# A hybrid decoder block on one core: the order of the projection blocks and the spread of the time-mixing steps

## The chip, the core and the metric

The kernel runs on one core of a Trainium2 chip. The metric is the device time of one execution in microseconds (us). Engines are TensorE (PE, with its weight loads as PEld), VectorE (DVE), ScalarE (ACT), GpSimd (POOL) and SyncE (SP), whose queue issues most DMAs. The granted clock of TensorE is given as a share of full speed.

## What is computed

A decoder block for a sequence of 2048 positions and a width of 1024, in float32. One projection feeds two groups of heads: eight heads of RWKV-7 time mixing (a recurrence over time with a 64 x 64 state per head) and four heads of differential attention. Their outputs are concatenated and projected, and a gated MLP with a causal convolution follows.

```python
# D_MODEL 1024, SEQ 2048, 8 time-mixing heads of 64, 4 attention heads of 2 x 64, D_FF 2816, CONV_WIDTH 3
def rwkv7_mix(p, mu, ...):
    ...
    xs = p + (token_shift(p) - p) * mu
    r, k, v, w_lo, a_lo, g_lo = jnp.split(xs, cuts, axis=-1)
    decay = jnp.exp(-DECAY_SCALE * jax.nn.sigmoid(w_decay0 + jnp.tanh(w_lo) @ w_decay_up))
    a = jax.nn.sigmoid(w_iclr0 + a_lo @ w_iclr_up)
    g = jax.nn.sigmoid(g_lo) @ w_gate_up
    ...
    def step(state, inp):
        r_t, w_t, k_t, v_t, kk_t, a_t = inp
        sa = jnp.einsum('bhvk,bhk->bhv', state, -kk_t)
        state = (state * w_t[:, :, None, :]
                 + sa[..., None] * (kk_t * a_t)[:, :, None, :]
                 + v_t[..., None] * k_t[:, :, None, :])
        return state, jnp.einsum('bhvk,bhk->bhv', state, r_t)
    ...
    return y * g

def diff_attention(q, k, v, lam, slopes):
    ...
        s = jnp.einsum('bhcqd,bhckd->bhcqk', qblk.astype(jnp.float32), kh) * scale
        s = s - slopes[None, :, None, None, None] * dist
        s = jnp.where(dist >= 0, s, NEG_INF)
        pr = jax.nn.softmax(s, axis=-1)
        attn = pr[:, :, 0] - lam * pr[:, :, 1]
        return jnp.einsum('bhqk,bhkv->bhqv', attn, vh)
    ...

def reference(x, ...):
    ...
        xn = rms_norm(h, ln_attn_pre[l])
        proj = xn @ w_in[l]
        y_rwkv = rwkv7_mix(proj[..., :RWKV_COLS], ...)
        dq, dk, dv = jnp.split(proj[..., RWKV_COLS:], 3, axis=-1)
        ...
        o = diff_attention(dq, dk, dv, lam, slopes)
        o = rms_norm(o, diff_subln[l], eps=SUBLN_EPS) * (1.0 - lam_init)
        mix = jnp.concatenate([y_rwkv, o.reshape(B, S, DIFF_DIM)], axis=-1).astype(h.dtype)
        h = h + rms_norm(mix @ w_out[l], ln_attn_post[l])
        hn = rms_norm(h, ln_ffn_pre[l])
        u = causal_dwconv(hn @ w_up[l], conv_w[l], conv_b[l])
        gate, val = jnp.split(u, 2, axis=-1)
        f = (jax.nn.gelu(gate, approximate=True) * val) @ w_down[l]
        h = h + rms_norm(f, ln_ffn_post[l])
    return h
```

## The kernel before

**Products.** A float32 product is made of three matmuls with operands split into a high and a low part (L99, L100, L101; the weights are split in L92 and L93).

**Projections** (class Proj). The columns of w_in are taken in 26 blocks of 128: blocks 0 to 13 (NRW = 14) are time mixing's, blocks 14 to 25 (NDF = 12) attention's, three for each head. The sequence is taken in two halves of 1024 rows, since only one half of the normalized and transposed x (tiles xh and xl) is held at a time. `start` normalizes and transposes half 0 and runs blocks 0 and 1 as a pair; `prepare` normalizes one tile of half 1 and stores it to DRAM (xn); `second` loads these eight tiles, transposes and splits them (L84) into the same buffers. A block's results go to DRAM: rw for time mixing (with the token shift), qq, kk and vT for attention.

**Time mixing** (class Rwkv) works on 16 groups of 128 positions, in steps that a generator hands out, one per turn; there are TURNS = 132. A group g has `prepare` (4 turns: operands from rw, then the matrices M), `invert` (1: a chain of 62 dependent VectorE operations on tile X, L530 and L532, then DMAs through the DRAM tile xdr to M, bdx and x1t), `join` (1: matmuls into xp) and `scan` (2: matmuls rp, sp, yp and up, two chunks in a row, each on the state that the one before left). The steps of `post(g-1)` (gate, normalization, output) are run inside scan(g). After nine first turns the plan is, for each g: join(g), scan(g), prepare(g+2), invert(g+1). `need` is the highest group that the next step wants, so that it is not run before that group's half has been projected.

**Attention** (class Attn) runs 64 units, four heads of 16 query blocks of 128. `scores` of unit i are followed by `output` of unit i - LAG (LAG = 2). VectorE evicts the scores (E, L794), ACT takes the exponential, TensorE transposes E (tp, L827), ACT copies the result (at, L829) and TensorE multiplies by V (op, L833); POOL ends a unit (on, L840). PSUM holds four banks in one set (tag MM) and two sets of two (RA, RC). Time mixing uses the sets of two; units below ALONE = 40 take everything from the set of four, later units use RA for transposes and RC for outputs.

**The order before.** Half 0: blocks 0 to 13, then 14 to 25 with `prepare` of half 1 in the first eight of them; `second`; half 1: blocks 0 to 25. Through the attention blocks of half 0 and the time-mixing blocks of half 1 the generator gives 1.5 turns for each block (PER), from then on 3.5 (PER2), 81 in all when the projections end. The other 51 turns are spread evenly over the first SPREAD = 44 attention units. When the last turn is done the weights of the output projection are loaded and split (tiles wor, woh, wol) and the convolution's tables cvA and cvB are made.

The program is built with `schedule_with_timeline_sim=True`: a scheduler moves instructions within each engine's order, so the order of the code is a wish and not the final order. Each engine then runs its own rows in order.

Of the kernel before, what the change touches and what calls it, by code (L numbers as in the profile page):

```python
# [8 lines left out]
F32 = mybir.dt.float32  # L9
# [8 lines left out]
P = 128  # L18
D = 1024
S = 2048  # L20
KB = D // P
HALF = 1024
GRP = 512
NRW = 14
NDF = 12
# [100 lines left out]
class Proj:  # L126


    def __init__(self, tc, nc, cx, I, pool):
        self.tc, self.nc, self.cx, self.I, self.pool = tc, nc, cx, I, pool  # L130
        ps = cx.ps
        self.rk = ["k_k", "k_a", "ln_x_w", "ln_x_b"]
        self.gain = None
        self.carry = pool.tile([P, NRW], F32, name="carry", bufs=1)
        nc.vector.memset(self.carry, 0.0)
        self.w_in = I["w_in"][0].rearrange("(kb p) c -> p kb c", p=P)
        self.half = 0

    def tables(self):
        nc, cx, I = self.nc, self.cx, self.I  # L140
# [7 lines left out]

    def begin(self, half):
        self.half = half  # L150
        self.xh, self.xl = alloc_xhl(self.pool, f"x{half}")

    def load(self, t, first=None):

        nc, pool = self.nc, self.pool
        if first:
            xt = self.norm(t, first, 8)
        else:
            xt = pool.tile([P, D], F32, name=f"xn{t}", tag="xt", bufs=2)
            nc.sync.dma_start(xt, self.cx.xn[t])  # L160
        transpose_split(nc, self.cx, self.cx.ps, xt, self.xh, self.xl, t, *(RA if first else MM))

    def second(self):
        self.begin(1)
        for t in range(HALF // P):
            self.load(t)

# [8 lines left out]

    def prepare(self, t):

        xt = self.norm(HALF // P + t, self.pool, 2)
        self.nc.sync.dma_start(self.cx.xn[t], xt)  # L180

    def weights(self, cb):
# [893 lines left out]


TURNS = 2 * 4 + 1 + NGRP * 3 + (NGRP - 2) * 4 + NGRP - 1 + 4
PER, PER2, SPREAD = 1.5, 3.5, 44


def block_kernel(tc, I, out):
    nc = tc.nc
    cx = Ctx()
    with ExitStack() as st:
# [6 lines left out]
        cx.kk = dt("kk", [NH, 2, 130, S])  # L1092
        cx.vT = dt("vT", [NH, P, S])
        cx.mix = [dt(f"mix{g}", [8, P, GRP]) for g in range(S // GRP)]
        cx.xn = [dt(f"xn{t}", [P, D]) for t in range(HALF // P)]
        cx.h = dt("hres", [S, D])
        cx.hn = dt("hnorm", [HALF, D])
        setup_consts(tc, nc, cx)
# [3 lines left out]
        with pool("pj", "left") as pp:  # L1102
            pj = Proj(tc, nc, cx, I, pp)
            with pool("x0", "right") as xp:
                pj.start(xp)
            attn_consts(tc, nc, cx, I)
            cx.const = right.enter_context(pool("const2", "right"))
            rwkv_consts(tc, nc, cx, I)
            rw = Rwkv(tc, nc, cx, right.enter_context(pool("rk", "right")), cx.ps)
            steps = rw.steps()  # L1110
            need = next(steps)
            turns = 0
            for cb in range(2, NRW):
                pj.block(cb)
            block = lambda cb: lambda: pj.block(cb)
            work = [block(cb) for cb in range(NRW, NRW + NDF - 2)]
            for t in range(HALF // P):
                f = work[t]
                work[t] = lambda f=f, t=t: (f(), pj.prepare(t))
            work += [lambda: pj.pair(NRW + NDF - 2, NRW + NDF - 1), lambda: pj.second()]  # L1120
            work += [lambda: pj.pair(0, 1), lambda: None] + [block(cb) for cb in range(2, NRW + NDF)]
            due = NDF + NRW
            for i, f in enumerate(work):
                upto = PER * (i + 1) if i < due else PER * due + PER2 * (i + 1 - due)
                while turns < upto and (need < HALF // RG or i >= due):
                    need = next(steps)
                    turns += 1
                f()
# [39 lines left out]
```

## Time and profile before

| what | value |
|---|---|
| median of 3 runs | 3182.57 us (3182.32 to 3184.49) |
| profiled execution | 3163.65 us |
| its span | 3161.9 us |
| TensorE busy | 3027.9 us, 96% of the span |
| VectorE busy | 1912.3 us, 60% |
| ScalarE busy | 1168.6 us, 37% |
| last projection matmul | 828.18 us |
| last time-mixing matmul | 1348.16 us |
| last attention unit ends | 1498.95 us |

The program has four stretches: projections up to 828 us, with time mixing between their matmuls from about 190 us on; attention with the rest of time mixing up to 1349; attention alone up to 1499.6; then the output projection and the MLP. A share of busy time is an average over these, so each is read by itself below. In the timeline a row gives the start, the duration, the engine, the line, the operation, the tile written and the tiles read; a wait before it stands in brackets with what ended it.

### The profile page before, as it was taken

To read this page: it belongs to the slowest core of one execution; us is meant where nothing else is said; L and a number is where in the kernel's file an instruction comes from. 1 tells how busy PE (TensorE), PEld (TensorE's weight loads), DVE (VectorE), ACT (ScalarE), POOL (GpSimd) and SP (SyncE) were. 2 spreads that over 40 slices of the span, in tenths; PEclk is the share of its full clock that TensorE was granted. 3 is DMA by queue.
4 is the path that set the end of the run, shared out by engine and by line. 5 is a ranking of instruction groups with operands and counts; after the bars stand their busy time and mean duration, and the time that the engine had idled before them with its cause. 6 is when DMAs were issued, how large, how long until landed. Compare 5 with 4: busy or idle time off the path is not lost.

```text
span 3161.9 us, 46143 instructions
## 1 busy us (share of the span) xinstructions
PE 3027.9 (96%) x17347; PEld 2489.9 (79%) x17347; DVE 1912.3 (60%) x4898; ACT 1168.6 (37%) x2332; POOL 328.2 (10%) x441
## 2 busy tenths in 40 slices
PE   7999999999988898889999999999999999999998
PEld 6887778787767777778888888888887888888886
DVE  5246655566588787777555455555557465555556
ACT  4233323333365655577333222222224322222223
POOL 3000000010232323232000000000000000000002
PEclk9999999999899998989999999999999999999999
DMA  5346523345623525152444111111114211111112
GB/s 156 97 147 182 164 89 104 95 112 135 140 65 74 101 64 97 43 140 60 146 160 153 47 54 51 50 47 41 57 51 162 78 47 40 55 53 47 47 34 87
DMA packets 362208, 282.41 MB, mean 89 GB/s; under 512 B 96847, under 2 KB 308402, under 8 KB 361986
## 3 DMA queue, kind: packets, MB, share of 16 engines
q1 hardware_dynamic: 334898, 247.12, 26.6%
q0 software_dynamic: 24784, 28.16, 5.0%
q10 hardware_dynamic: 2304, 4.20, 0.4%
q8 instruction: 137, 2.24, 0.3%
q14 instruction: 85, 0.70, 0.1%
HBM read 204.72 MB, written 73.88 MB: 88 GB/s over the span
## 4 chain that ended last, share of the span: by engine, by line
PE 78%; DVE 6%; DMA 3%; ACT 1%; issue 1%; SPq 1%; POOL 0%; DVEq 0%; ACTq 0%; POOLq 0%
PE fp L99 10%; PE fp L101 10%; PE fp L100 10%; PE dn L100 5%; PE dn L99 5%; PE dn L101 5%; PE pp L100 4%; PE pp L99 4%; PE pp L101 4%; PE op L833 3%; PE po L99 2%; PE po L101 2%; PE po L100 2%; PE sp L789 1%; PE sp L790 1%
## 5 line engine op out<-in xcount | busy, mean ns | idle before, releaser
L1015 DVE TENSOR_TENSOR acc<-dn,acc 128x512 f32<-128x512 f32 x320 | 211.5, 687 | 224.4 <-PE dn L101 222.1
L99 PE MATMUL fp<-f1h,uh 128*128 128x512 f32 x704 | 275.4, 391 | 5.0 <-DVE fcarry L980 5.0
L101 PE MATMUL fp<-f1h,ul 128*128 128x512 f32 x704 | 275.3, 391 | 0.0
L100 PE MATMUL fp<-f1l,uh 128*128 128x512 f32 x704 | 275.3, 391 | 0.0
L100 PE MATMUL dn<-dl,gh 128*128 128x512 f32 x704 | 275.2, 391 | 0.0
L99 PE MATMUL dn<-dh,gh 128*128 128x512 f32 x704 | 272.4, 391 | 1.9 <-DVE acc L1015 1.9
L99 PE MATMUL fp<-f0h,uh 128*128 128x512 f32 x704 | 274.2, 389 | 0.0
L101 PE MATMUL fp<-f0h,ul 128*128 128x512 f32 x704 | 274.1, 389 | 0.0
L100 PE MATMUL fp<-f0l,uh 128*128 128x512 f32 x704 | 274.0, 389 | 0.0
L101 PE MATMUL dn<-dh,gl 128*128 128x512 f32 x704 | 264.0, 391 | 0.0
L93 DVE TENSOR_TENSOR ul<-ur,uh 128x1024 fp32r<-128x1024 f32 x88 | 107.7, 1225 | 188.1 <-ACT uh L92 188.1
L794 DVE TENSOR_SCALAR_CACHE_REDUCE E<-sp 128x512 f32<-128x512 f32 (+3 forms) x320 | 187.4, 605 | 41.7 <-PE sp L792 23.9
L976 DVE SCALAR_TENSOR_TENSOR u<-fp,cvA,u 128x511 f32<-128x511 f32 x176 | 131.3, 746 | 119.8 <-ACT u L974 119.8
L833 PE MATMUL op<-V,at 128*128 128x128 f32 x1088 | 161.5, 294 | 29.2 <-ACT at L829 28.4
L92 ACT CAST dh<-dr 128x1024 fp32r<-128x1024 f32 x44 | 44.4, 1047 | 386.8 <-PE dn L101 383.9
L833 PEld LDWEIGHTS op<-V,at 128*128 128x128 f32 x1088 | 143.6, 202 | 42.6 <-ACT at L829 35.9
L100 PE MATMUL pp<-x1l,wh 128*128 128x512 f32 x416 | 168.7, 406 | 0.0
L99 PE MATMUL pp<-x1h,wh 128*128 128x512 f32 x416 | 168.3, 405 | 0.0
L99 PE MATMUL pp<-x0h,wh 128*128 128x512 f32 x416 | 167.9, 404 | 0.1
L803 ACT ACTIVATE E<-E,asc 128x1024 f32<-128x1024 f32 (+7 forms) x160 | 153.6, 963 | 37.1 <-DVE asc L799 36.6
L100 PE MATMUL pp<-x0l,wh 128*128 128x512 f32 x416 | 167.3, 402 | 0.0
L101 PE MATMUL pp<-x0h,wl 128*128 128x512 f32 x416 | 167.0, 402 | 0.0
(303 smaller groups left out, 6697.5 us busy)
## 6 DMA issues: line engine op xcount, KB each, us to landing
ur<-in_w_up SPq DMA_DIRECT2D x88, 512.0 KB, 3.8
wr<-in_w_in SPq DMA_DIRECT2D x52, 512.0 KB, 4.3
dr<-in_w_down SPq DMA_DIRECT2D x44, 512.0 KB, 3.4
rw<-e SPq DMA_DIRECT2D x56, 256.0 KB, 3.9
x<-in_x SPq DMA_DIRECT2D x16, 512.0 KB, 6.1
qq<-e SPq DMA_DIRECT2D x64, 128.0 KB, 2.3
kk<-e SPq DMA_DIRECT2D x64, 128.0 KB, 2.4
ab<-adr SPq DMA_DIRECT2D x64, 128.0 KB, 2.7
```

The source lines that it names most:

```text
L92: nc.scalar.copy(wh, wr)
L93: nc.vector.tensor_tensor(wl, wr, wh.bitcast(F32), op=ALU.subtract)
L99: nc.tensor.matmul(out, lh(kb), rh(kb), start=(kb == 0), stop=False)
L100: nc.tensor.matmul(out, lh(kb), rl(kb), start=False, stop=False)
L101: nc.tensor.matmul(out, ll(kb), rh(kb), start=False, stop=(kb == n - 1))
L789: nc.tensor.matmul(sp[:, 0:n], qa[:, c, qs], ka[:, c, 0:n], start=True, stop=False)
L790: nc.tensor.matmul(sp[:, 0:n], qx[0:66, c, qs], kb[0:66, c, 0:n], start=False, stop=not last)
L794: nc.vector.tensor_scalar(e[ch * GRP // EW][:, eo:eo + n], sp[:, 0:n], -1.0, None, op0=ALU.mult, op1=ALU.min, accum_out=mx[:, ch:ch + 1])
L803: nc.scalar.activation(e[i][:, 0:n], e[i][:, 0:n], AF.Exp, bias=nm, scale=-1.0, accum_out=z)
L833: nc.tensor.matmul(op, at[:, q, :], v[:, q, :], start=(kb == 0), stop=(kb == qb))
L976: stt(u[:, 1:GRP], pp[:, 0:GRP - 1], w1(b), u[:, 1:GRP], op0=ALU.mult, op1=ALU.add)
L1015: nc.vector.tensor_tensor(acc[:, t, ds_], po, acc[:, t, ds_], op=ALU.add)
```

## The change

Half 0 runs only its 14 time-mixing blocks first (with `prepare` of half 1 in eight of them); then `turn(1)` loads half 1, which runs its 14 time-mixing blocks and its 12 attention blocks; then `turn(0)` loads half 0 a second time, and its 12 attention blocks end the projections. For that `start` also stores the eight tiles of half 0 to xn, which now has 16 tiles. `uses` only numbers names. Turns are given out from the first block of half 1 on: 57 (FIRST) up to the end of its time-mixing blocks, 126 (DONE) at the end of all blocks; the last six go to the first six attention units (SPREAD).

```diff
--- before.py
+++ after.py
@@ -134,7 +134,7 @@
         self.carry = pool.tile([P, NRW], F32, name="carry", bufs=1)
         nc.vector.memset(self.carry, 0.0)
         self.w_in = I["w_in"][0].rearrange("(kb p) c -> p kb c", p=P)
-        self.half = 0
+        self.half = self.uses = 0
 
     def tables(self):
         nc, cx, I = self.nc, self.cx, self.I
@@ -148,6 +148,7 @@
 
     def begin(self, half):
         self.half = half
+        self.uses += 1
         self.xh, self.xl = alloc_xhl(self.pool, f"x{half}")
 
     def load(self, t, first=None):
@@ -155,13 +156,16 @@
         nc, pool = self.nc, self.pool
         if first:
             xt = self.norm(t, first, 8)
+            nc.sync.dma_start(self.cx.xn[t], xt)
         else:
-            xt = pool.tile([P, D], F32, name=f"xn{t}", tag="xt", bufs=2)
-            nc.sync.dma_start(xt, self.cx.xn[t])
+            n = self.half * (HALF // P) + t
+            xt = pool.tile([P, D], F32, name=f"xn{self.uses}_{n}", tag="xt", bufs=2)
+            nc.sync.dma_start(xt, self.cx.xn[n])
         transpose_split(nc, self.cx, self.cx.ps, xt, self.xh, self.xl, t, *(RA if first else MM))
 
-    def second(self):
-        self.begin(1)
+    def turn(self, half):
+
+        self.begin(half)
         for t in range(HALF // P):
             self.load(t)
 
@@ -176,7 +180,8 @@
 
     def prepare(self, t):
 
-        xt = self.norm(HALF // P + t, self.pool, 2)
+        t += HALF // P
+        xt = self.norm(t, self.pool, 2)
         self.nc.sync.dma_start(self.cx.xn[t], xt)
 
     def weights(self, cb):
@@ -1076,7 +1081,7 @@
 
 
 TURNS = 2 * 4 + 1 + NGRP * 3 + (NGRP - 2) * 4 + NGRP - 1 + 4
-PER, PER2, SPREAD = 1.5, 3.5, 44
+FIRST, DONE, SPREAD = 57, 126, 6
 
 
 def block_kernel(tc, I, out):
@@ -1092,7 +1097,7 @@
         cx.kk = dt("kk", [NH, 2, 130, S])
         cx.vT = dt("vT", [NH, P, S])
         cx.mix = [dt(f"mix{g}", [8, P, GRP]) for g in range(S // GRP)]
-        cx.xn = [dt(f"xn{t}", [P, D]) for t in range(HALF // P)]
+        cx.xn = [dt(f"xn{t}", [P, D]) for t in range(S // P)]
         cx.h = dt("hres", [S, D])
         cx.hn = dt("hnorm", [HALF, D])
         setup_consts(tc, nc, cx)
@@ -1110,18 +1115,24 @@
             steps = rw.steps()
             need = next(steps)
             turns = 0
-            for cb in range(2, NRW):
+            for cb in range(2, NRW - 2):
                 pj.block(cb)
+                if cb - 2 < HALF // P:
+                    pj.prepare(cb - 2)
+            pj.pair(NRW - 2, NRW - 1)
+            pj.turn(1)
             block = lambda cb: lambda: pj.block(cb)
-            work = [block(cb) for cb in range(NRW, NRW + NDF - 2)]
-            for t in range(HALF // P):
-                f = work[t]
-                work[t] = lambda f=f, t=t: (f(), pj.prepare(t))
-            work += [lambda: pj.pair(NRW + NDF - 2, NRW + NDF - 1), lambda: pj.second()]
-            work += [lambda: pj.pair(0, 1), lambda: None] + [block(cb) for cb in range(2, NRW + NDF)]
-            due = NDF + NRW
+            pair = lambda cb: [lambda: pj.pair(cb, cb + 1), lambda: None]
+            last = NRW + NDF - 2
+            work = pair(0) + [block(cb) for cb in range(2, NRW)]
+            due = len(work)
+            work += [block(cb) for cb in range(NRW, last)] + pair(last)
+            work += [lambda: (pj.turn(0), pj.pair(NRW, NRW + 1)), lambda: None]
+            work += [block(cb) for cb in range(NRW + 2, NRW + NDF)]
             for i, f in enumerate(work):
-                upto = PER * (i + 1) if i < due else PER * due + PER2 * (i + 1 - due)
+                upto = FIRST * min(i + 1, due) / due
+                if i >= due:
+                    upto += (DONE - FIRST) * (i + 1 - due) / (len(work) - due)
                 while turns < upto and (need < HALF // RG or i >= due):
                     need = next(steps)
                     turns += 1
```

From L200 on, lines of the changed kernel stand five below those of before (L607 is L612, L560 is L565, L789 is L794). In the rows that follow, pp is a projection block, up, rp, sp_N, yp with one number belong to the scan of that group, gp, mp and vs to post, n and bo to prepare, xp to join; sp_ABC of a score row is made of head and query block and chunk, as tp and op of transposes and outputs.

TensorE at the end of projections, before: behind the last rows of block 25 of half 1 stand the last products of scan 7 (up_7) and the join of group 8.

```order
L99 MATMUL pp_25_1_8169<-x1h_3129,wh_25_8137 128x512
L100 MATMUL pp_25_1_8169<-x1l_3131,wh_25_8137 128x512
L101 MATMUL pp_25_1_8169<-x1h_3129,wl_25_8138 128x512
L607 MATMUL up_7_7266<-sav_6345,bkt_6355 64x64 x8
L644 MATMUL gp_7287<-sg_5630,gup 128x128 x4
L366 MATMUL n_9_7322<-rT_556,sel 128x128 x4
L560 MATMUL xp_7597<-ident,x1t_7595 128x32 x4
L590 MATMUL rp_8_7688<-state_588,AR_6769 64x64 x8
L565 MATMUL xp_7597<-x_8_7598,bda 128x32 x4
```

TensorE at the same place after: the block is that of half 0 (x0h), and behind it stand up_10 and the join of group 11.

```order
L99 MATMUL pp_25_1_10541<-x0h_8054,wh_25_10509 128x512
L100 MATMUL pp_25_1_10541<-x0l_8056,wh_25_10509 128x512
L101 MATMUL pp_25_1_10541<-x0h_8054,wl_25_10510 128x512
L468 MATMUL bo_8013<-t_b_8010,ones_551 128x512
L612 MATMUL up_10_7908<-sav_6925,bkt_6935 64x64 x8
L649 MATMUL gp_7929<-sg_6138,gup 128x128 x4
L371 MATMUL n_12_7964<-rT_572,sel 128x128 x4
L565 MATMUL xp_8453<-ident,x1t_8451 128x32 x4
L595 MATMUL rp_11_8472<-state_604,AR_7349 64x64 x8
L570 MATMUL xp_8453<-x_11_8454,bda 128x32 x4
```

Three more groups stand ahead of this point than before, five are still to come (11 to 15).

TensorE some 130 rows later, after: the last scores of unit 6 (sp_611), then the join of group 12 and its scan.

```order
L794 MATMUL sp_611_11045<-ka_10878,qa_11021 128x384
L795 MATMUL sp_611_11045<-kb_10879,qb_11022 128x384
L797 LDWEIGHTS identb
L797 MATMUL sp_611_11045<-caus,identb 128x128
L565 MATMUL xp_8981<-ident,x1t_8979 128x32
L595 MATMUL rp_12_9072<-state_604,AR_7949 64x64 x8
L565 MATMUL xp_8981<-ident,x1t_8979 128x32 x3
L570 MATMUL xp_8981<-x_12_8982,bda 128x32 x4
L573 MATMUL xp_8981<-bdx,x_12_8988 32x128 x4
L600 MATMUL sp_12_9082<-kv_8352,M_8016 64x64 x8
L632 MATMUL mp_9093<-ybv_7351,ones_551 128x512
L609 MATMUL yp_12_9098<-AR_7949,state_604 64x64 x8
```

From here on no row of attention stands on TensorE for 108 rows, up to this place (gp and vs are the last rows of post 15, tp_50 and op_5 belong to unit 5, sp_700 to unit 7):

```order
L639 MATMUL vs_10846<-onesmc,t_a_10808 128x2 x4
L649 MATMUL gp_10982<-sg_9808,gup 128x128 x4
L366 MATMUL vs_10846<-ident,rs_ln_10851 8x128
L371 MATMUL vs_10846<-rT_573,sel 128x128 x4
L48 MATMUL cvA_ps<-ident,cvA_st 128x128
L48 MATMUL cvB_ps<-ident,cvB_st 128x128
L832 MATMUL tp_50_11118<-ident,E_500_10952 128x128 x4
L838 MATMUL op_5_11117<-V_10578,at_50_11123 128x128 x4
L832 MATMUL tp_51_11129<-ident,E_500_10952 128x128 x2
L794 MATMUL sp_700_11146<-ka_10573,qa_11021 128x512
```

Before, the last row of post 15 stood among the outputs of units 43 and 44 (head 2, query blocks 11 and 12):

```order
L827 MATMUL tp_111_13989<-ident,E_1100_13748 128x128 x4
L644 MATMUL gp_13909<-sg_12318,gup 128x128 x4
L827 MATMUL tp_112_14000<-ident,E_1101_13749 128x128 x4
L827 MATMUL tp_120_14073<-ident,E_1200_13856 128x128 x4
L833 MATMUL op_11_13977<-V_12417,at_110_13983 128x128 x4
L833 MATMUL op_11_13977<-V_12842,at_111_13994 128x128 x4
```

The time-mixing rows of groups 12 to 15 have moved out from between the attention units to a place of their own ahead of unit 7.

VectorE in that place, after: in the chain of group 13 (X, xtmp) stands the addition kv_12, which reads rp_12, the first product of scan 12.

```order
L535 TENSOR_TENSOR xtmp_9503<-X_8783,ab_8778 128x66
L537 TENSOR_TENSOR X_8783<-X_8783,xtmp_9503 128x3x22
L535 TENSOR_TENSOR xtmp_9503<-X_8783,ab_8778 128x63
L597 TENSOR_TENSOR kv_8352<-rp_12_9072,kv_8352 128x256
L537 TENSOR_TENSOR X_8783<-X_8783,xtmp_9503 128x3x21
L535 TENSOR_TENSOR xtmp_9503<-X_8783,ab_8778 128x60
```

Forty rows of the chain stand behind this addition.

Behind the last time-mixing row the eight splits of the output weights (wol) stand on VectorE ahead of the first eviction of unit 7 there; before, five of them stood ahead of the evictions of unit 45 and three among these.

TensorE in `turn(0)`, after (xt are the transposes of x; vt and bt belong to prepare 8):

```order
L84 MATMUL xt_0_8075<-ident,xn_1_8073 128x128 x3
L84 MATMUL xt_1_8082<-ident,xn_1_8073 128x128 x4
L570 MATMUL xp_5921<-x_7_5922,bda 128x32 x4
L497 MATMUL vt_5798<-ident,vv_5614 128x128 x4
L506 MATMUL bt_8_5808<-ident,BK_5622 128x128 x4
L84 MATMUL xt_0_8091<-ident,xn_2_8089 128x128 x4
L84 MATMUL xt_1_8098<-ident,xn_2_8089 128x128 x4
```

As in `second` before, time-mixing rows stand between the transposes; in `turn(1)` there are none, since no turn has been given out by then.

## Rows read from the trace of the kernel before

**Rows 1.** Windows: busy us (x instructions) of PE, PEld, DVE, ACT, POOL; PEclk, DMA, GB/s.

```profile
600.00:828.40 228.40, 228.40 (x1818) 183.43 (x1816) 142.73 (x418) 80.23 (x168) 22.69 (x21) 1.00 0.46 115
828.40:913.00 84.60, 72.04 (x586) 59.77 (x586) 59.74 (x205) 39.67 (x106) 33.24 (x45) 0.78 0.58 119
828.40:1349.00 520.60, 456.04 (x4026) 382.41 (x4026) 400.88 (x1477) 296.92 (x753) 152.66 (x202) 0.90 0.40 82
1366.00:1386.00 20.00, 18.76 (x51) 13.24 (x52) 19.16 (x53) 12.13 (x19) 1.50 (x2) 0.50 0.24 76
1413.00:1499.60 86.60, 81.37 (x592) 71.91 (x590) 69.17 (x253) 68.73 (x173) 27.71 (x43) 1.00 0.22 63
```

**Rows 2.** Windows, projection matmuls alone (tile pp): PE busy (count), clock, DMA share, GB/s.

```profile
600.00:828.40 228.40, 154.34 (x606) 1.00 0.46 115
```

**Rows 3.** PE timeline, end of projections: start, us, engine, line, operation, tiles, count.

```profile
827.02 0.39 PE L99 MATMUL pp<-x1h,wh 128*128 128x512 f32 x1
...
828.18 0.40 PE L101 MATMUL pp<-x1h,wl 128*128 128x512 f32 x1
```

**Rows 4.** PE timeline, last block of half 0, `second`, first matmul of half 1.

```profile
372.76 0.39 PE L101 MATMUL pp<-x0h,wl 128*128 128x512 f32 x1
...
380.69 1.94 PE L84 MATMUL xt<-ident,xn 128*128 128x128 f32 x8 [1.88 <-DMA xn<-xn]
...
397.49 1.09 PE L84 MATMUL xt<-ident,xn 128*128 128x128 f32 x8 [1.46 <-DMA xn<-xn]
...
398.34 0.48 PE L99 MATMUL pp<-x1h,wh 128*128 128x512 f32 x1
```

**Rows 5.** DVE timeline, first and last operation of two inverse chains.

```profile
788.84 0.19 DVE L530 TENSOR_TENSOR xtmp<-X,ab 128x31 f32<-128x31 f32 x1 [2.68 <-DMA ab<-adr]
...
809.49 0.18 DVE L532 TENSOR_TENSOR X<-X,xtmp 128x8 f32<-128x8 f32 x1
...
863.52 0.18 DVE L530 TENSOR_TENSOR xtmp<-X,ab 128x31 f32<-128x31 f32 x1
...
913.05 0.18 DVE L532 TENSOR_TENSOR X<-X,xtmp 128x8 f32<-128x8 f32 x1
```

**Rows 6.** SP and PE timelines: load of x1t behind an inverse, join of its group.

```profile
924.51 0.43 SPq L547 DMA_DIRECT2D x1t<-xdr  x1
...
926.82 0.24 PE L560 MATMUL xp<-ident,x1t 32*128 32x32 f32 x1
```

**Rows 7.** PE timeline, first rp and last up of two scans.

```profile
831.17 0.68 PE L590 MATMUL rp<-state,AR 64*64 64x64 f32 x16
...
868.95 0.69 PE L607 MATMUL up<-sav,bkt 128*64 128x64 f32 x16
...
1299.31 0.91 PE L590 MATMUL rp<-state,AR 64*64 64x64 f32 x12
...
1328.72 0.45 PE L607 MATMUL up<-sav,bkt 128*64 128x64 f32 x8
```

**Rows 8.** PE waits: operation, cause, us in total, times, longest; 828.4:1349, then 1413:1499.6.

```profile
PE op L833 <- ACT at L829: 25.0, 19, 7.2
...
PE op L833 <- ACT at L829: 2.4, 5, 1.3
```

**Rows 9.** PE timeline, last time-mixing matmul and the second table of the convolution.

```profile
1348.16 1.06 PE L644 MATMUL gp<-sg,gup 128*128 128x128 f32 x8
...
1365.91 0.45 PE L48 MATMUL cvB_ps<-ident,cvB_st 128*128 128x128 f32 x1 [8.09 <-DMA cvB_st<-in_conv_b]
```

**Rows 10.** POOL timeline, last operation of units 47, 52, 58 and 63.

```profile
1413.53 0.61 POOL L840 TENSOR_SCALAR on<-osb,asc 128x128 f32<-128x128 f32 x1
...
1428.27 0.61 POOL L840 TENSOR_SCALAR on<-osb,asc 128x128 f32<-128x128 f32 x1
...
1461.12 0.61 POOL L840 TENSOR_SCALAR on<-osb,asc 128x128 f32<-128x128 f32 x1
...
1498.95 0.61 POOL L840 TENSOR_SCALAR on<-osb,asc 128x128 f32<-128x128 f32 x1
```

## The prediction

> **What bounds the kernel now.** I read the windows first, since the change only touches the stretch from the first projection to the end of attention. From 600 to 828.4 us TensorE is busy for the whole window at full clock [rows 1]: projections with time mixing between them, so whatever is added there costs its full TensorE time. From 828.4 to 1349 us, where attention units and the last time-mixing groups share the chip, TensorE is busy 456 of 520.6 us, and the granted clock averages 0.90, between its two levels of 1.2 and 2.4 GHz: waits and low clock decide, not the amount of work. From 1413 to 1499.6 (the last head alone) it is 81.4 of 86.6 us at clock 1.00: almost bound by TensorE again. So the question is how long each of three stretches becomes: projections, time mixing that is left over, attention that is left over. The timelines then give the places: the last projection matmul is at 828.18 [rows 3], the last time-mixing matmul at 1348.16 [rows 9], the last unit's last operation at 1498.95 [rows 10]. What follows (output projection, MLP) is the same work in the same order; I carry it over unchanged.
>
> **What the order says.** The code asks for 126 of the 132 turns before attention. The scheduled order does not deliver them: at the last projection matmul of the changed kernel the scan of group 10 is ending, where before it was that of group 7. Three groups more are done, five (11 to 15) are still to do. Scan 11 goes beside units 0 to 6. Then come 108 rows of TensorE with time mixing alone (scans 12 to 15), and only then unit 7 and output 5. I price these pieces one after the other, from the end of projections.
>
> **1. Projections, longer by three groups and a turn.** In 600 to 828.4 us, 606 projection matmuls were issued [rows 2]; in an undisturbed run five of them take 827.02 to 828.18, 0.232 us each [rows 3], so they fill 141 us and the other 87 us belong to about four groups: 21.8 us each. Three groups: +65 us. The extra turn: second() takes from 372.76 to 398.34, 25.6 us [rows 4]; eight transposes take 1.09 us there, so 64 take 8.7, and the rest is time mixing and waits for the loads (1.88 and 1.46 us are the shown ones). turn(0) has time mixing between its transposes too: between 8.7 us (all waits covered) and 25.6 (none), I take 17. turn(1) has none beside it, unlike second(): 0 to 17 us dearer, I take 4, as only the shown waits grow. Eight more stores and eight more loads of 512 KB stand in SP's queue; a descriptor such as x1t's takes 0.43 us to issue [rows 6], so eight cost at most 3.4 us where they delay the x loads at the start, and I take 0 since those loads lead by several tiles. Projections end at 828.4 + 65 + 21 = **914** us, with bounds of 902 and 932.
>
> **2. From there to the join of group 12.** Before, group 9's inverse ends at 913.05 and its join starts at 926.82, 98 us after the end of projections [rows 5, 6]. VectorE's rows between the two points are nearly the same in both orders (187 before, 182 after, the same 20 or so evictions of scores among them), and TensorE stands at clock 0.78 there [rows 1]. So the join of group 12 starts at 914 + 98 = 1012 (92 to 100 after the end).
>
> **3. Time mixing alone.** The trace of before has no such stretch, so it is bounded from its links. The inverse is a VectorE chain of 62 dependent operations: 20.6 us where VectorE has little else (788.84 to 809.49), 49.5 us among score evictions (863.52 to 913.05) [rows 5]. From its end to the join 13.8 us go by in DMAs [rows 5, 6]. A scan, from its first rp to its last up, takes 29 us (1299.31 to 1328.72) or 38 us (831.17 to 868.95, at the lower clock) [rows 7]. In the order the last 40 rows of group 13's chain stand behind the addition that waits for scan 12's first rp: to the join of 13 it takes some 4 + 40 × 0.225 + 13.8, 28 us with the row or two of scan 12 between. Group 14's chain stands among scan 13 and the preparation of 15: 38 + 20.6 + 13.8 = 72 us. Group 15 again as 13, 28 us, and its scan with the last two post steps 30 us. Sum **158** us; bounds: four light links of 28, 112 us, and 38 + 72 + 38 + 38 = 186. I take the middle value since the stretch has the little-loaded VectorE of the light chain but the stop-and-go TensorE of scan 8. Time mixing then ends at 1012 + 158 = **1170**; before, 1349.
>
> **4. Attention behind it.** Before, 150.6 us remain at 1349 (to 1499.6), with outputs 43 to 63 still to do, the wait for the convolution's table (8.09 us) [rows 9] and the loading of the output weights among them; all that comes again. Outputs 5 to 42 come on top. The last head, alone, gives their pace: 85.4 us for a head (1413.53 to 1498.95), 70.7 for its blocks 5 to 15 (from 1428.27), 47.6 for its blocks 0 to 10 (to 1461.12) [rows 10]; 70.7 + 85.4 + 47.6 = 203.7 us. Two additions. Units below ALONE = 40 take all PSUM tiles from one set of four banks, and this number was not moved: in the shared stretch their output matmuls waited 25.0 us for ACT's copies, in the last head, with its own banks, 2.4 us [rows 8]. For the 38 units I take 15 us (bounds 0 and 55, twice the rate of the shared stretch). And the eight splits of the output weights stand on VectorE ahead of unit 7's evictions, where only outputs 5 and 6 are left to cover them, and before there were 11 and 12: +9 us (0 to 9). Rest: 150.6 + 203.7 + 15 + 9 = **378**.
>
> **Sum.** 1170 + 378 = 1548 against 1499.6: +48.7 us. The profiled execution took 3163.65 us, so it becomes some 3212; the median of runs stood 18.9 us above it, and the same shift on the median gives 3182.57 + 48.7 = 3231 us.
>
> **The same total from TensorE's side.** Nearly all matmul work is the same, so the loss is idle and slow time. Before, in 828 to 1349, 64.6 us idle and a tenth of the clock; after, 158 us of time mixing hold the TensorE work of four groups (87 us), so 71 us idle at once, plus 17 us of transposes and waits. The part saved is the shared stretch at clock 0.90 becoming attention alone at 1.00. Both sides are of the same size, which is why the range is wide on both sides of the sum.
>
> **What the notes say.** The Trainium skill, page Perfetto Trace Analysis, section Optimization Strategy, says that where the most contended engine changes over time, interleaving those regimes may help. That speaks against this change: it takes a chain bound by latency out of attention. But projections are such a regime as well, and three groups do move there; by the rule, those three are gained (rival A) and the four left alone are lost (the forecast), and the rows of the order decide which is more. The same page, section Matmul Optimizations, wants all 8 PSUM banks in use; units 7 to 39 alone use four of them, and no row of before shows a unit alone on four banks.
>
> **Rivals.** *A, faster:* with nothing beside it, time mixing runs on its light links. Then projections end at 905, the join of 12 comes 92 us later, the tail takes 112, and attention runs at the last head's pace with no bank stalls and covered splits, 354 us: 1463, -36 us, 3146. For it: the light chain of 20.6 us is in the trace. Against it: TensorE stood at clock 0.50 from 1366 to 1386 after a wait [rows 1], and a tail of short matmuls and long waits invites that. It decides below a tail of 109 us with my other terms (1499.6 - 378 - 1012), or of 133 with attention's additions at nothing. *B, nothing:* a tail of about 115 to 130 us, with the additions between: within 6 us of before. *C, dearer attention:* units 7 to 39 on four banks stall at twice the shared rate, 55 in place of 15 us, and the tail comes to 170: 3283. For it: ALONE stays 40 though nothing else wants the other banks. Against it: without time mixing ACT copies sooner. *D, the change works as the code asks:* 126 turns done in projections. Then projections would end at 828.4 + 7.5 × 21.8 + 21 = 1013, and attention alone, 4 × 85.4 + 15 + 35 for the weights, at 1405: 3088. The order excludes it (scan 11 stands behind the last projection), unless the rows that the engines take in order overlap far better than I think.
>
> **How the numbers follow.** Forecast (+10 to +90 us) 0.70; C and worse (over +90) 0.10; B 0.06; A 0.13; D 0.01. What a measurement of this kernel can tell from no change is about 0.2%, 6 us. So faster 0.14, same 0.06, slower 0.80. The range leaves out the far half of A with D, and the far end of C (all upper bounds together would be 3317): 3165 to 3290. Likeliest: 3231.
>
> **What would show it.** In the profile after: the last projection matmul near 914; the join of group 12 near 1012; from there some 158 us in which no score matmul runs, VectorE's inverse chain on the chain of waits, and a granted clock well under 1 in it; the convolution's tables behind it near 1170; the last unit near 1548; waits of output matmuls for ACT of some 15 us. It is wrong if the tail is under 109 us, if scores run inside it, or if projections stretch by more than 104 us.

## The result, and the profile after

The changed kernel takes 3295.59 us (median of 4 runs, 3291.88 to 3301.02) against 3182.45 us for the kernel before: 1.0359 times as long, interval 1.034 to 1.0378, +113 us. The forecast had the sign, but +48.7 us, and its range ended at 3290. The profiled execution took 3301.02 us, near its median; that of before (3163.65) lies 18.8 us below its own. So the two traces differ by 137 us, and some 24 of these are only the choice of the executions.

In the trace of the changed kernel the stretches are read from five windows: from the end of projections to the join of group 12; time mixing alone; to the end of unit 5; to the end of unit 40; to the end of unit 63. The columns are those of [rows 1].

```profile
926.50:1026.40 99.90, 71.36 (x545) 58.84 (x544) 60.55 (x213) 37.60 (x101) 31.23 (x41) 0.67 0.57 111
1026.40:1172.00 145.60, 119.79 (x1028) 95.38 (x1028) 80.50 (x266) 35.80 (x89) 13.55 (x10) 0.58 0.16 35
1172.00:1199.60 27.60, 9.61 (x45) 7.40 (x45) 15.10 (x27) 13.89 (x22) 2.75 (x5) 0.58 0.55 191
1199.60:1484.80 285.20, 223.34 (x1404) 186.74 (x1403) 179.06 (x645) 169.12 (x425) 82.43 (x128) 0.92 0.34 64
1484.80:1637.00 152.20, 139.55 (x981) 122.12 (x979) 116.60 (x418) 113.01 (x282) 48.77 (x74) 0.97 0.33 69
```

The TensorE timeline gives the ends of the first two stretches: the last projection matmul, the joins of groups 12 to 15 (first row of each), the last gate product and the two tables of the convolution.

```profile
926.54 0.39 PE L101 MATMUL pp<-x0h,wl 128*128 128x512 f32 x1
...
1026.42 0.31 PE L565 MATMUL xp<-ident,x1t 32*128 32x32 f32 x1 [19.75 <-DMA x1t<-xdr]
...
1055.19 0.43 PE L565 MATMUL xp<-ident,x1t 32*128 32x32 f32 x4
...
1117.29 0.31 PE L565 MATMUL xp<-ident,x1t 32*128 32x32 f32 x1 [7.04 <-DMA x1t<-xdr]
...
1142.58 0.60 PE L565 MATMUL xp<-ident,x1t 32*128 32x32 f32 x4 [1.78 <-DMA x1t<-xdr]
...
1170.01 2.05 PE L649 MATMUL gp<-sg,gup 128*128 128x128 f32 x8
...
1181.98 0.45 PE L48 MATMUL cvA_ps<-ident,cvA_st 128*128 128x128 f32 x1 [7.58 <-DMA cvA_st<-in_conv_w]
...
1190.20 0.45 PE L48 MATMUL cvB_ps<-ident,cvB_st 128*128 128x128 f32 x1 [7.77 <-DMA cvB_st<-in_conv_b]
```

Up to here the forecast holds: projections to 926.5 (forecast 914), join of 12 at 1026.4 (1012), time mixing done at 1172 (1170), with no attention row in the tail and the granted clock at 0.58 in it. The last operation of the last unit on POOL answers to the last of [rows 10]:

```profile
1636.88 0.61 POOL L845 TENSOR_SCALAR on<-osb,asc 128x128 f32<-128x128 f32 x1
```

From 1172 on 465 us go by, where 378 were forecast. So nearly all of the miss between the traces (87 of 89 us) lies behind the part that was hard to price, in attention alone. TensorE's waits from unit 5 to unit 40 (1199.6 to 1484.8; operation, cause, us in total, times, longest) say for what:

```profile
PE op L838 <- ACT at L834: 38.4, 37, 2.7
PE vp L757 <- DMA vtl<-vT: 6.7, 1, 6.7
PE tp L832 <- DVE E L819: 5.2, 6, 1.6
```

The output matmuls wait 38.4 us for ACT's copies in these 285 us; in the last head of before, whose units have their own banks, it was 2.4 in 86.6 [rows 8].

### The profile page after: what moved, and what is told of

Its sections match the earlier page's. It is cut to its first block, busy times and chain, and to the rows that moved or that the text cites. A ratio compares the mean times of both kernels' runs of the same rounds, so it can differ in the third digit from the quotient of the medians.

```text
span 3299.3 us, 46381 instructions
## 1 busy us (share of the span) xinstructions
PE 3092.1 (94%) x17411; PEld 2538.5 (77%) x17411; DVE 1948.9 (59%) x4914; ACT 1180.6 (36%) x2348; POOL 324.5 (10%) x441
## 4 chain that ended last, share of the span: by engine, by line
PE 56%; DVE 4%; ACT 2%; DMA 1%; issue 1%; POOL 0%; DVEq 0%; SPq 0%; ACTq 0%; POOLq 0%
PE fp L99 10%; PE fp L101 9%; PE fp L100 9%; PE dn L100 5%; PE dn L99 5%; PE dn L101 5%; PE op L838 3%; PE po L99 2%; PE po L101 2%; PE po L100 2%; PE sp L794 1%; PE sp L795 1%; DVE E L799 1%; ACT E L808 1%; PE tp L832 1%
## 5 line engine op out<-in xcount | busy, mean ns | idle before, releaser
L101 PE MATMUL pp<-x1h,wl 128*128 128x512 f32 x416 | 170.8, 411 | 0.0
```

The lines of the kernel that those rows point to most:

```text
L101: nc.tensor.matmul(out, ll(kb), rh(kb), start=False, stop=(kb == n - 1))
```

## The experiments

The theory after the result, *banks*: the units below ALONE = 40 take scores, transposes and outputs from one set of four PSUM banks although time mixing has left the others; that, and not the tail, is what the forecast had too small. The rival, *heads*: units of the first heads are dearer anyway, because of a low clock after the tail and of loads. The medians of the kernel before in the shared comparisons below are 3176 to 3178 us.

**Own banks from unit 7.**

```diff
-ALONE = 40
+ALONE = 7
```

> The changed kernel with ALONE = 7 in place of 40: units 7 to 39 also take their transposes and outputs from their own two sets of two PSUM banks; nothing else differs. In the changed kernel the outputs of units 5 to 39 took 270 us (1199.6 to 1470) where the last head's pace of before would give some 185. Theory 'banks': the 85 us are the one set of four banks that scores, transposes and outputs share, and lower clock that follows from its pauses; then this run comes 65 to 85 us below the changed kernel, at 3210 to 3230 us, its outputs 5 to 39 take 185 to 205 us and the waits of output matmuls for ACT (44.9 us) fall below 10. Rival 'heads': units of the first heads are dearer whatever the banks, because of a low clock that the time-mixing tail leaves behind and of loads of V and q; then it stays within 15 us of the changed kernel, at 3280 to 3300.

Measured: 3223.43 us (1.014 times before, 1.0113 to 1.0167), 72 us below the changed kernel. The scheduled order is nearly the same up to unit 7. The window from the end of unit 5 to that of unit 40, the wait of the output matmuls in it, and the window to the end of unit 38:

```profile
1196.10:1417.60 221.50, 203.89 (x1443) 178.50 (x1443) 178.72 (x669) 169.63 (x439) 87.12 (x131) 0.97 0.47 84
...
PE op L838 <- ACT at L834: 3.4, 9, 1.1
...
1196.10:1401.40 205.30, 187.69 (x1323) 163.89 (x1323) 165.01 (x620) 156.56 (x405) 83.28 (x125) 0.97 0.49 87
```

285.2 us have become 221.5. TensorE is idle 17.6 us in place of 61.9, and its nearly equal number of matmuls is busy 203.9 us in place of 223.3, at a granted clock of 0.97 in place of 0.92. So about 44 of the 64 us were waits and 20 slower matmuls, which the waits column does not show. *Heads* falls. The 185 to 205 us expected were for the stretch up to 1470, by POOL's rows the end of unit 38 (1468.7); up to there this trace takes 205.3 us, the upper end, and 10.8 of them are two waits for loads of q.

Behind unit 7 the order of TensorE's rows is another as well, since the scheduler makes it for the banks that it has. On four banks 38 of the 88 groups of output matmuls in the window stand directly behind transposes, and TensorE waits for ACT's copy; with own banks 18 of 88 do, and the others have scores between (first two rows: the changed kernel; the others: own banks from unit 7):

```profile
1455.84 0.61 PE L832 MATMUL tp<-ident,E 128*128 128x128 f32 x4
1457.12 1.16 PE L838 MATMUL op<-V,at 128*128 128x128 f32 x8 [0.68 <-ACT at L834]
...
1384.78 0.72 PE L832 MATMUL tp<-ident,E 128*128 128x128 f32 x5
1385.25 0.48 PE L794 MATMUL sp<-ka,qa 128*128 128x512 f32 x1
...
1387.34 1.05 PE L838 MATMUL op<-V,at 128*128 128x128 f32 x8
```

So the run shows the price of the constant, that is, of the banks together with the order that the scheduler makes of them. What one order would cost on four banks and on eight, no run shows.

**The kernel before on four banks to the end.**

```diff
-ALONE = 40
+ALONE = 64
```

> The kernel before with ALONE = 64 in place of 40: its last 24 units, too, share one set of four banks. Theory 'banks': 2.4 us a unit (85 us over 35 units of the changed kernel) for the 20 or so units that run without time mixing, so 45 to 60 us above the kernel before, 3227 to 3242 us. Rival 'heads': the last head runs at its pace on four banks as well, within 8 us of before, 3175 to 3190.

Measured: 3224.34 us (1.0146, 1.0119 to 1.0173), +48 us, just under the 3227 expected as the lower end. It is nearly the price of *banks* in the other kernel, where no tail, no reload and no new order of the blocks is in play. Window and wait of its last head (units 48 to 63):

```profile
1433.50:1556.20 122.70, 95.68 (x604) 79.81 (x603) 76.73 (x267) 72.77 (x178) 25.24 (x40) 0.93 0.17 49
...
PE op L833 <- ACT at L829: 18.9, 17, 2.7
```

Against it the same head of before, from the end of unit 48 to that of unit 63 (its wait is the second of [rows 8]):

```profile
1415.30:1499.00 83.70, 79.07 (x573) 69.75 (x572) 66.87 (x243) 66.47 (x167) 25.47 (x39) 1.00 0.22 63
```

39 us for 15 units, 2.6 us each, 22 of it idle time and 17 busy time at clock 0.93 in place of 1.00.

**The new order with the old turns.** FIRST = 45, DONE = 81, SPREAD = 44, that is, turns nearly as before:

```diff
-FIRST, DONE, SPREAD = 57, 126, 6
+FIRST, DONE, SPREAD = 45, 81, 44
```

> The new order of the blocks with its second reload, but the turns as before: 45 up to the end of the time-mixing blocks of half 1, 81 at the end of the projections, the other 51 over 44 attention units. It prices the new order by itself. If the reload costs what the prediction took for it (21 us with the turn that has no time mixing beside it) and the shared stretch is as before: 3195 to 3210 us. If the reload hides behind time mixing: 3178 to 3188. If the order is what costs most of the 113 us: over 3240.

Measured: 3200.22 us (1.0073, 1.0044 to 1.0101), +24 us. In its order scan 8 is ending at the last projection matmul, one group more than before and two fewer than in the changed kernel, and that matmul stands here:

```profile
890.06 0.40 PE L101 MATMUL pp<-x0h,wl 128*128 128x512 f32 x1
```

So two groups cost 926.5 - 890.1 = 36.4 us of projections, 18.2 each, and, if the third group costs the same, the new order by itself 890.1 - 828.2 - 18.2 = 43.7 us of them. The projections end 62 us later than before; at the end of attention 35 us of these are left (1534.0 against 1499.0), by the medians 24, since a group fewer is left to do there.

**The reload alone.** The kernel before loads, transposes and splits half 1 a second time, ahead of its attention blocks:

```diff
             due = NDF + NRW
+            work[-NDF] = lambda f=work[-NDF]: (pj.second(), f())
```

> The kernel before with half 1 loaded, transposed and split a second time ahead of its attention blocks: 8 loads, 64 transposes and 16 evictions more, no block moved and no turn moved in the code. It prices the reload by itself. The prediction's term was 17 us (bounds 8.7 and 25.6); the trace of the changed kernel shows 33 us without projection matmuls at this place, with time mixing beside. 3188 to 3203 by the prediction's term; 3205 to 3220 if the whole gap is lost; under 3184 if time mixing fills it.

Measured: 3196.57 us (1.0063, 1.0044 to 1.0082), +18.8 us. The last projection matmul moves from 828.18 to 841.97:

```profile
841.97 0.40 PE L101 MATMUL pp<-x1h,wl 128*128 128x512 f32 x1
```

The forecast's 17 us for a reload stand.

**The spread alone.** The changed kernel with its last turns over 44 units:

```diff
-FIRST, DONE, SPREAD = 57, 126, 6
+FIRST, DONE, SPREAD = 57, 126, 44
```

> The changed kernel with SPREAD = 44 in place of 6: the last six turns (as the code counts) are spread over 44 units, so the scheduled order sets scans 11 to 15 among units 0 to 24, with no stretch of time mixing alone; units 25 to 39 then run alone on four banks. If the stretch of time mixing alone costs what the trace shows (146 us with the TensorE work of four groups, 87 us, in it, so some 60 us) and the units on four banks 2.4 us each (15 of them in place of 33): 40 to 100 us below the changed kernel, 3195 to 3255. If the tail costs nothing because the work only moves: 3250 to 3290, by the banks alone.

Measured: 3201.73 us (1.0071, 1.0048 to 1.0094), 94 us below the changed kernel. Units 28 to 40 of it run without time mixing and still on four banks: 98.2 us, at a granted clock of 0.81.

```profile
1290.60:1388.80 98.20, 75.85 (x433) 64.21 (x431) 52.84 (x198) 52.89 (x136) 30.93 (x49) 0.81 0.40 73
```

**Both.** SPREAD = 44 and ALONE = 28:

```diff
-ALONE = 40
+ALONE = 28
-FIRST, DONE, SPREAD = 57, 126, 6
+FIRST, DONE, SPREAD = 57, 126, 44
```

> The changed kernel with SPREAD = 44 and ALONE = 28: time mixing is spread over the attention units (as in the run with SPREAD = 44 alone, 3201.7 us) and units 28 to 39, which then run without time mixing, get their own banks. Theory: the two causes add. Units 28 to 40 took 98 us with SPREAD 44 (1290.6 to 1388.8); at the pace of the run with own banks from 7 (units 28 to 40: 1345.9 to 1417.6, 72 us) they take 26 us less: 3170 to 3185, and 35 to 55 us below the run with own banks and the tail (3223.4), which is then the price of a tail alone. Rival: the last groups collide with units 28 on in the sets of two banks, and nothing is gained: 3195 to 3215.

Measured: 3154.58 us, 0.9929 times before (0.9906 to 0.9952): faster than both kernels, and by more than expected. The same units 28 to 40:

```profile
1271.70:1342.20 70.50, 60.80 (x414) 52.36 (x414) 56.26 (x193) 55.06 (x139) 34.53 (x49) 0.93 0.79 170
```

The stretch is 28 us shorter, where the theory said 26; the stretch ahead of it, on four banks in both kernels, is another 19 us shorter (344.4 against 363.3), which the theory didn't forecast. Up to about 1210 the two traces run level to within 4 us; the difference arises in the last units ahead of unit 28. There the orders differ, and with SPREAD alone the weights of the output projection are loaded and split (wol) there, here only from 1321 on:

```profile
1254.56 1.23 DVE L93 TENSOR_TENSOR wol<-wor,woh 128x1024 fp32r<-128x1024 f32 x1
...
1320.94 1.22 DVE L93 TENSOR_TENSOR wol<-wor,woh 128x1024 fp32r<-128x1024 f32 x1
```

Whether these loads are the cause was not tested. The run with ALONE = 7, which has the tail and own banks, lies 3223.4 - 3154.6 = 69 us above this one. So 141 us lie between the changed kernel and this one, 72 at the banks and 69 at the tail if the banks are set right first. The other way round it is 94 at the spread and 47 at the banks, since spreading also shortens the stretch that is alone on four banks.

**Half the dose.** SPREAD = 44 and ALONE = 34:

> The changed kernel with SPREAD = 44 and ALONE = 34, between the runs with 40 (3201.7 us) and 28 (3154.6 us). Theory 'banks': each unit without time mixing pays about 3.9 us on four banks, so six of the twelve give half, 3170 to 3188. If only the end of time mixing against the switch matters (a collision at one place), it is like one of the two ends.

Measured: 3169.79 us (0.9981, 0.9966 to 0.9996), just under the lower end expected. The three runs with SPREAD = 44 fall in the order of the switch, 3201.7 at 40, 3169.8 at 34, 3154.6 at 28, but not evenly: 32 us for the six units 34 to 39, 15 for the six below. In the traces units 28 to 40 take 98.2, 80.9 and 70.5 us, that is 17 and 10 us less by the switch. Another 15 of the 32 lie ahead of unit 28, where both kernels are on four banks and the order is nearly the same: the last 190 matmuls there run at a granted clock of 0.75 with SPREAD alone, beside the weights (131 GB/s), and at 1.00 in this run, where the weights come later (38 GB/s; first row SPREAD alone, second this run).

```profile
1242.00:1290.60 48.60, 38.40 (x190) 32.18 (x190) 35.29 (x94) 29.56 (x60) 8.76 (x12) 0.75 0.41 131
...
1240.00:1275.20 35.20, 28.38 (x190) 23.48 (x190) 26.13 (x86) 21.84 (x52) 7.12 (x11) 1.00 0.14 38
```

So the 3.9 us a unit of the expectation hold more than the banks.

**The old order with the new spread.**

```diff
-PER, PER2, SPREAD = 1.5, 3.5, 44
+PER, PER2, SPREAD = 1.5, 7.25, 6
```

> The old order of the blocks (no second reload) with the changed spread: 1.5 turns a block as before, then 7.25 a block to 126 turns, and six units for the last six. The scheduled order shows that the projections do not take more time mixing in for that (scan 7 ends behind them, as in the kernel before) and that scans 9 to 15 stand alone, behind unit 4. At the changed kernel's 36 us a group (1026.4 to 1172, four groups) these seven take 255 us from the join of group 9, about 926, and end near 1180, as in the changed kernel (1172), with the same units on four banks behind it. So 3290 to 3315 if the three groups that the new order takes in only pay for its longer projections; 3340 to 3400 if they are a net gain of the new order.

Measured: 3355.89 us (1.0563, 1.0525 to 1.0601), 60 us above the changed kernel, in the band that stood for a net gain of the new order. The forecast end of time mixing (1180) was missed: it comes at 1215. Joins of groups 12 and 13, 14 and 15 (first rows), and the last gate product:

```profile
1047.70 0.50 PE L560 MATMUL xp<-ident,x1t 32*128 32x32 f32 x4
...
1113.62 0.31 PE L560 MATMUL xp<-ident,x1t 32*128 32x32 f32 x1 [6.25 <-DMA x1t<-xdr]
...
1141.70 0.63 PE L560 MATMUL xp<-ident,x1t 32*128 32x32 f32 x4
...
1191.20 0.28 PE L560 MATMUL xp<-ident,x1t 32*128 32x32 f32 x1 [12.08 <-DMA x1t<-xdr]
...
1214.43 0.80 PE L644 MATMUL gp<-sg,gup 128*128 128x128 f32 x5
```

Groups alone go by in pairs, a short step (28 us) and a long one (66 and 50 us), as the forecast worked out from the order (28 and 72). A pair costs 78 to 94 us alone in this trace, and 36 inside the projections: the difference is what the new order gains for each two groups that it takes in, against the 43.7 us that it costs.

**The old order with spread and banks.** PER2 = 7.25, SPREAD = 44, ALONE = 28:

> The old order with 126 turns asked for by the end of projections, SPREAD = 44 and ALONE = 28: no second reload, no tail alone, own banks from unit 28. In the scheduled order the projections end with scan 7, as before, and time mixing ends near unit 35. If spreading and banks carry over: 3150 to 3180 us, at or below the kernel before. If time mixing and units 28 to 35 collide in the sets of two banks: 3185 to 3210.

Measured: 3208.72 us (1.0091, 1.0063 to 1.012): the collision. Here the last two groups are still to be joined when the switch comes. On POOL unit 27 and unit 28 end 99 us apart. Between these ends TensorE has the joins of groups 14 and 15, the second behind a wait of 20.95 us, and no output matmul before 1320.5:

```profile
1228.88 0.62 POOL L840 TENSOR_SCALAR on<-osb,asc 128x128 f32<-128x128 f32 x1
...
1243.91 0.31 PE L560 MATMUL xp<-ident,x1t 32*128 32x32 f32 x1
...
1296.97 0.28 PE L560 MATMUL xp<-ident,x1t 32*128 32x32 f32 x1 [20.95 <-DMA x1t<-xdr]
...
1320.51 4.31 PE L833 MATMUL op<-V,at 128*128 128x128 f32 x24
...
1327.99 0.61 POOL L840 TENSOR_SCALAR on<-osb,asc 128x128 f32<-128x128 f32 x1
```

The order set the rest of time mixing ahead of the outputs of the first unit that wants the same banks. Scores of the next units still stand between its rows up to 1273; from there to 1320 time mixing is alone, a short tail. So the switch has a price on either side: too late, four banks; too early, a tail. Of the old order no setting with a later switch was run.

**Two more settings of the changed kernel.**

> The changed kernel with SPREAD = 28 and ALONE = 24: in the scheduled order time mixing ends at unit 23, where it ended at unit 35 in the run with 44 and 28 (3154.6 us), and own banks begin at unit 24. From the run with SPREAD = 44 alone (3201.7) to that with ALONE = 28 as well, 12 units gained 47 us, 3.9 us a unit. Theory 'banks': four units more on their own banks, 10 to 16 us less, 3138 to 3148. Rival 'chain': the last groups' inverses then find too few units to cover them (a short tail), 3155 to 3185.

Measured: 3164.81 us (0.9964, 0.9946 to 0.9981): in the range of the rival *chain*, 10 us above the run with 44 and 28 though four more units have their own banks. Its mechanism isn't shown: in the trace rows of attention stand among those of time mixing to the end, with no more than 5.2 us between two of them, so there is no tail. The weights are split early here too, from 1248 on.

> The new order with 106 turns asked for by the end of the projections in place of 126, the rest over 40 units, ALONE = 36. The scheduled order at the end of projections is the same as in the changed kernel (scan 10 just ends there), so it shows whether the number asked for matters beyond what the order delivers. By the banks (units 36 to 39 alone on four sets less than in the run with 40) and the spread: 3170 to 3190, between the runs with SPREAD 44 and ALONE 34 and 40; under 3160 if the later last groups cover better.

Measured: 3176.93 us (1.0001, 0.9986 to 1.0016), between the runs with ALONE 34 and 40. Asking for 106 turns or 126 makes no difference that these runs show, and the scheduled order is the same at the end of projections; but three constants change at once here, so the number of turns isn't priced by itself.

## Why the prediction was wrong

Step by step, in the trace of the changed kernel:

- **End of projections**: 926.5 for 914, inside its bounds, but by two errors that partly cancel. (The upper bounds of its terms add up to 936 and not to 932.) Three groups cost 3 × 18.2 = 55 us in place of 65; why the 87 us of [rows 2] gave too much for a group stays open. The term for the turns was 21 us and measures 43.7. The reload in it was right, as priced in the kernel before (13.8 us of projections, +18.8 in all). What was too small is the rest, some 30 us. One part is seen: `turn(1)` takes 188.5 to 218.15 and TensorE stands at clock 0.68, where 25.6 us of `second` [rows 4] held more time mixing. Nor is it bare, as the text ahead of the prediction has it: rows of the first preparation stand among its transposes. The forecast took 4 us for losing the cover, with 17 as its bound. What the remainder is was not separated.

```profile
188.50:221.00 32.50, 22.14 (x108) 18.38 (x107) 24.03 (x45) 15.82 (x32) 4.24 (x4) 0.68 0.64 201
...
193.22 0.61 PE L421 MATMUL zw<-twx,lora 65*128 65x128 f32 x4
```

- **To the join of group 12**: 99.9 us for 98. Carrying over a stretch whose rows on VectorE are the same was right.
- **Time mixing alone**: 146 us for 158, with links of 28.8, 62.1, 25.3 and 29.5 for 28, 72, 28 and 30. The bounds from separate links, put together along the order, held for a stretch that the trace of before does not contain. That the first link came out at 28 is partly luck: 0.225 us for a row of the chain stands in no row shown ([rows 5] has 20.6 us for 62, or 0.33), the 40 rows took 12.2 us for 9, the DMAs behind them 14.8 for 13.8, and what stands ahead of them 1.8 for 4. Rival A (112 us) didn't come, but not for the reason given against it: at a clock of 0.58 three of the four links are about as light as its 28 us. The 34 us above it are the one long link, in which the order sets the chain of group 14 among scan 13 and the preparation of 15.

```profile
1028.16 0.21 DVE L537 TENSOR_TENSOR X<-X,xtmp 128x63 f32<-128x63 f32 x1
...
1040.21 0.17 DVE L537 TENSOR_TENSOR X<-X,xtmp 128x8 f32<-128x8 f32 x1
```

- **Attention behind it**: 465 us for 378. This is the step that failed, and in it the term for the units on four banks: 15 us, bounds 0 to 55. By the run with own banks it is 64 us in the trace and 72 in the medians, above the upper bound. Two things were wrong with it. Its rate came from the shared stretch, where 25.0 us of this wait fall on some 42 outputs, 0.6 us each; alone it is 38.4 us on 35, 1.1 each. That time mixing fills TensorE in the shared stretch and nothing does so in the units alone is the likely reason, not a shown one. And only the named wait was counted, while the slower matmuls that come with the pauses are a third of the price. By its own rate the term would have been some 23 us, and twice that 45, not 55. The measured row of a unit alone on four banks was missing, the prediction said so, and still took a value in the lower part of its bounds.
- **The rest of that stretch**: with own banks it takes 394 us (1167.4 to 1561.2) where the other terms give 363. Outputs 5 to 42 take 229 in place of 203.7 (q waits of 10.8 us among them; the first heads do not quite reach the last head's pace), and weights and tables with nothing beside them add 5. That is the remaining 30 us.
- **From the trace to the median**: the shift by the medians is 113 us, by the traces 137. The forecast was made on a profiled execution that lies at the fast end of its runs; that was taken as a plain offset of 18.9 us on both kernels and is not one.

Rival C named the four banks and gave 3283; its banks were still too cheap and its tail too dear. Of the idea behind the change the runs show that the new order can be worth having: three groups cost 55 us inside the projections and much more alone, and with the spread and the switch set for it the kernel is 0.7% faster than before. How far the old order would come with as many settings tried was not run. The changed kernel loses because it moved the end of time mixing from unit 42 to unit 7 and left ALONE at 40, and because six units are too few to cover five groups.

The Trainium skill, page Perfetto Trace Analysis, section Matmul Optimizations, asks for all 8 PSUM banks to be used. The runs agree, and price it here: 2.6 us a unit in the last head of the kernel before.

## What to carry to other kernels

When a change moves the point at which one kind of work ends, look for every constant that was set to that point (here the unit from which attention takes the freed banks) and price the stretch in which it is now wrong by a trace of that very state, not of a stretch where other work stood beside it. A chain bound by latency is cheap inside matmul-bound work and dear alone, so ask of the scheduled order, not of the code's counts, how much of it is left and what covers that. And a stall on TensorE costs more than its wait: add the slower matmuls around it.

## What the runs showed of the hardware

In units 5 to 40 of the changed kernel TensorE's granted clock is 1.00 over the first 60 us, with waits of up to 2.0 us between the matmuls and TensorE busy for 49.3 us. It falls behind a wait of 2.54 us: from 1268 to 1270 it is 0.50, the lower of the two levels.

```profile
1199.60:1259.60 60.00, 49.31 (x327) 40.49 (x325) 43.80 (x153) 37.90 (x94) 13.05 (x21) 1.00 0.16 42
...
1266.44 1.75 PE L838 MATMUL op<-V,at 128*128 128x128 f32 x8 [2.54 <-ACT at L834]
...
1268.00:1270.00 2.00, 2.00 (x9) 1.81 (x9) 1.65 (x3) 0.00 (x0) 0.00 (x0) 0.50 0.00 0
```

Over the whole 285 us, in which waits go up to 6.7 us, it averages 0.92, with own banks 0.97, and in the tail of short matmuls 0.58. The pauses are paid twice: 44 us idle, 20 us in longer matmuls (an output matmul averages 304 ns against 282, a transpose 293 against 273).
